# Unit order, selection rounds and gate sums moved between the input projection and the mixers of a two-layer hybrid decoder

## The chip, the core and the metric

The kernel runs on one NeuronCore of a Trainium2 chip. Its engines are TensorE (PE in the profile, with its weight loads shown apart as PEld), VectorE (DVE), ScalarE (ACT) and GpSimd (POOL); SyncE (SP) issues most of the DMAs. The metric is the device time of one launch in microseconds (us). Each engine executes its instructions in one fixed order.

## The reference, cut to what matters

Two layers. In each, one input projection makes the columns of four parallel groups of heads, the groups are mixed over the tokens, one output projection and a gated MLP follow. There are 1024 prompt tokens and 8 sequences of 4 sample tokens with 2048 cached tokens each.

```python
h = rmsnorm(x, norm1_g) * (1 + sc1) + sh1
p = split_cols(h @ w_in)                  # lru, diff, dsa, idx, gla columns
# A: RG-LRU recurrence over p["lru_x"], gated by p["lru_gate"]
# B: differential attention, q and k rotated (rope)
# C: sparse attention: index scores, exact 256 largest keys per query, q and k rotated
idx, valid = dsa_select(iq, iw, ik, q_pos, k_pos, 256)
o_c = dsa_attend(q_c, k_c[idx], v_c[idx], valid)
# D: gated linear attention; b is the running sum of log alpha in a chunk
b = cumsum(log_a / 16);  att = sum_k q k exp(b_t - b_s);  o = att @ v + (q exp(b)) @ S
x = x + g1 * (concat(o_a, o_b, o_c, o_d) @ w_out)
x = x + g2 * mlp(...)
```

The samples run B and C over their paged caches, and C needs its own selection of 256 keys per sample query.

## The kernel before

All activations of the projection are float32 split in two parts, so that 24 matmuls make one output tile. The projection runs unit by unit, 256 columns of `w_in` each. A `nat_unit` (queries, keys and values that later steps want by token) runs 9 token tiles through `dense_n` (L471); its queries and keys are rotated by `rope`: two VectorE instructions (L499 and L503) and two on GpSimd (L501, L502). A `t_unit` (features on partitions) runs 6 pieces of 384 or 288 columns through `dense_c` (L451). The units before were, in order: misc, idx_q, lru_x, lru_gate, dsa_q, dsa_k, dsa_v, diff_q, diff_k, diff_v, gla_v, gla_q with gla_k, gla_g.

Between the tiles `background()` lets side streams take steps: `idx_prompt` (index scores of the prompt), then `topk_prompt`, which finds the exact 256th largest score of each query by bisection with counts over all keys (L799 on VectorE, the upper 16 bits into `tkb`, the lower 16 into `tku`) and ends with the mask `mk` (L872); also `sample_index`, `rg_lru` and `sample_select`, the samples' own bisection, here called sel, whose round on VectorE holds the pair L967 and L969 (`srep`). `mk` of the last block, 128x1024, is the end of `topk_prompt`.

After the projection come the mixers. `gla()` (linear attention) goes first, in two halves of the prompt: `decays(half)` loads the 16 gate columns `ga`, multiplies by `wa2` (L1727), forms the log (ACT, L1730 to L1733, DVE L1734, L1736) and the running sum `gb` (scan, L1743); `operands(half)` loads q, k and v and makes the terms `gl`; `chunks(half)` does the attention in chunks of 128 tokens: PE L1700, and DVE L1711 into `gatt`. With it runs `samples()`, half a step for each of gla's steps, and sel, a step for every second. Each of the 16 sequences of the samples (8 for diff, 8 for dsa) has a group of keys (`samp_keys`: PE transposes L1334, scores L1340, mask L1343) and of values (`samp_values`, L1363; `samp_merge`). Then `prompt()` runs the prompt's attention with 0.8 sample steps for each of its own, and what is left of the samples runs alone; the last `out_t` (L1263) ends the prompt's part. The output projection (L451) follows and needs all the mixes.

The order of the instructions on an engine is not that of the code: a scheduler places each when its inputs are expected, and the streams decide what is available. Two further constants matter:

```python
SELH = 1    # projection: one step of sel per tile
SELM = 2    # gla: one step of sel per two of gla's
KA = 0.5    # sample steps per step of gla
while kind == "dsa" and advance(sel): yield     # samples(): the rest of sel
```

Of the kernel before, what the change touches and what calls it, by code (L numbers as in the profile page):

```python
# [22 lines left out]
D = 1024  # L23
# [21 lines left out]
SELH = 1  # L45
# [26 lines left out]
def _const_tables():  # L72
    """Tables and 0/1 masks that depend on shapes alone, one float32 array of 128 rows."""
# [67 lines left out]
def trunk(ctx, tc, io, out, dbg=None, depth=DEPTH, stop=99):  # L141
# [31 lines left out]
    def advance(gens, n=1):  # L173
        """n steps of the first streams of the list that are not done; False when none is left."""
# [9 lines left out]
    def pipeline(gens, depth):  # L184
        """the streams one after another, up to depth of them at once, a step of each per step, oldest first."""
# [20 lines left out]
    def evac(dst, src, ratio=(1, 1)):  # L206
        """PSUM to SBUF on ScalarE or VectorE in turns."""
# [91 lines left out]
            # half the convolution: silu(2 z) = z (1 + tanh(z))  # L299
# [17 lines left out]
    def ada(adap, l, u0, u1, nb=2, ne=1, nk=8):  # L317
        """units of 512 columns of the modulation, in pieces of nk * 128 rows and 1024 / nk columns."""
# [27 lines left out]
    def add_square(x, k, c, acc, tmp):  # L346
        """acc += x^2 for the features of tile k, chunk c of the tokens."""
# [13 lines left out]
    def rstd_chunk(get, acc, c):  # L361
# [3 lines left out]
        # 1 / sqrt(v), v = sum / D + eps: ScalarE's value, then a Newton step  # L365
# [9 lines left out]
    def split(hi, lo, y, bias, k):  # L375
        """hi + lo = y + bias, lo on VectorE or GpSimd in turns."""
# [8 lines left out]
    def norm_chunk(get, x, acc, c, A, mod, base, hi, lo):  # L385
        """hi + lo = modulated norm of x, chunk c of the tokens."""
# [16 lines left out]
    def part(wp, c, z):  # L403
        """tile for part z of [features, tokens], chunk c of the tokens."""
# [7 lines left out]
    def raw_piece(rp, aps, width, i, n, nr):  # L412
        """rows of piece i of n of a [1024, width] block of weights; aps: list of (column, AP)."""
# [12 lines left out]
    def unit(wp, rp, aps, width, n=2, first=None):  # L426
        """hi and lo of a block of weights, [128, 8, width]."""
# [10 lines left out]
    def split2(parts_, c, g, raw):  # L438
        """the parts of two tiles of features, chunk c of the tokens."""
# [4 lines left out]
    def dense_c(w, j, h, c, order=range(8)):  # L444
        """out^T[m, t] = sum_k w[k, m] h[k, t] for 128 columns m and chunk c of the tokens."""
# [16 lines left out]
    def dense_n(w, i, h):  # L462
        """out[t, m] = sum_k h[k, t] w[k, m] for token tile i, 256 columns."""
# [12 lines left out]
    def add_residual(x, m, c, p, gate, mod):  # L476
        """x += gate * p for 128 features m and token chunk c."""
# [11 lines left out]
    def rope(dst, src, i, n, d, tmp, rope_t):  # L489
        """dst[n, heads * d] = rotary of src (SBUF, natural rows of token tile i)."""  # L490
# [15 lines left out]
    # the scores' scales go into the queries, with their signs turned (minima for maxima)  # L506
# [60 lines left out]
    # the prompt's query blocks 2.. of the index: ScalarE counts by signs (2 * count - n) in those of ACT_BLK  # L567
# [11 lines left out]
    # rows of the caches: 4 tokens each; token (g*128+p)*4+j of sequence b lies in row idx[p, g, b]  # L579
# [33 lines left out]
    for l in range(depth):  # L613
# [8 lines left out]
        stt["gla_a"] = dr.tile([16, T], F32, name=f"stt_a{l}")  # L622
        mixg = [dr.tile([2, 128, T], F32, name=f"mix{l}_{k}") for k in range(4)]
# [9 lines left out]
        # ================= input projection =================  # L633
# [5 lines left out]
        def background():  # L639
# [5 lines left out]
            if count[0] % SELH == 0:  # L645
                advance(sel)
# [56 lines left out]
        def dup(dst, src, nh, d, key):  # L703
            """[n, nh, d] in two float32r parts, laid out (hi, hi, lo, lo) for queries, (hi, lo, hi, lo) for keys."""
# [7 lines left out]
        def stack_t(dst, srcs, idr=None):  # L712
            """dst[:, i*128:] = transpose of srcs[i], four to a PSUM bank."""
# [57 lines left out]
        def topk_prompt(tk):  # L771
            """Bisection over the bits of the float, the upper 16 first on the truncated values (order and
            comparisons with such thresholds are kept by truncation), then the lower 16 of those that share
            the upper ones. mk becomes 0 where chosen, -NEG elsewhere; ties in the order of the keys."""
# [32 lines left out]
            # thresholds of at least 0 end in zeros: the bfloat16 moved up by less than its spacing never equals  # L807
            # one, nor do those below 0, which end in ones. No bias of ScalarE's is subnormal.
# [390 lines left out]
        while advance(late) or advance(side):  # L1199
            pass  # L1200
# [1042 lines left out]
```

## Time and profile before

| | |
|---|---|
| median of 3 runs (lowest, highest) | 3935.86 us (3932.43, 3936.16) |
| the profiled execution | span 3915.6 us, 66494 instructions |
| PE / PEld busy | 3549.8 / 3202.2 us |
| DVE / ACT / POOL busy | 2461.3 / 1510.5 / 1387.5 us |
| layer 0, input projection from the top-k's first count | 275 to 562 us |
| layer 0, gla / prompt's mixers / samples alone | 562 to 743 / to 1058 / to 1077 us |
| layer 1, projection from the first count, gla | 2213 to 2500, to 2664 us |

Only the span has times of single instructions; the median lies 20.3 us above it. Busy shares are means over stages that have different limits, so the rows further below are taken by stage.

### The profile page before, as it was taken

Reading aid. Unit: us, or ns where it says so; the run is one execution under the profiler, and the core shown is the slowest. Engines: PE = TensorE matmul, PEld = TensorE weight load, DVE = VectorE, ACT = ScalarE, POOL = GpSimd, SP = SyncE. Lnnn points to the kernel's source line nnn. Section 1 sums busy time; section 2 is a strip of 40 time slices with the busy share of each in tenths; the row PEclk is TensorE's granted clock in tenths of the full one; section 3 lists DMA queues with packets and bytes.
Section 4 is the critical chain, followed back from the end, with each engine's and each line's share of the span. In section 5 each row is a group of like instructions: output and inputs, shape, how many; then the busy total and the mean of one; then the engine's idle time right before and its main releaser. Section 6 shows DMA issues by size and latency. Waiting matters only on the chain.

```text
span 3915.6 us, 66494 instructions
## 1 busy us (share of the span) xinstructions
PE 3549.8 (91%) x26004; PEld 3202.2 (82%) x26004; DVE 2461.3 (63%) x5614; ACT 1510.5 (39%) x3058; POOL 1387.5 (35%) x1241
## 2 busy tenths in 40 slices
PE   5998867899898999999979988688997899999998
PEld 3887765577788999999979877556786899999997
DVE  6379989676445454445553999996753545555555
ACT  4345644376533211211243556535763322112122
POOL 2344226534233222222323642564333222323231
PEclk7999988999999999999989999899998999999999
DMA  6542334546431333321113222546546011111111
GB/s 223 158 129 87 112 116 144 181 131 187 165 103 44 98 103 94 96 76 44 55 65 89 87 87 79 155 150 195 150 155 207 28 44 44 49 39 54 44 44 56
DMA packets 351155, 407.77 MB, mean 104 GB/s; under 512 B 93455, under 2 KB 294909, under 8 KB 350682
## 3 DMA queue, kind: packets, MB, share of 16 engines
q1 hardware_dynamic: 311930, 265.09, 22.5%
q0 software_dynamic: 38912, 138.43, 11.1%
q8 instruction: 205, 3.36, 0.4%
q14 instruction: 108, 0.88, 0.1%
HBM read 354.32 MB, written 58.04 MB: 105 GB/s over the span
## 4 chain that ended last, share of the span: by engine, by line
PE 66%; DVE 19%; DMA 4%; ACT 4%; issue 4%; POOL 1%; SPq 1%; another core or an unknown queue 0%; DVEq 0%; ACTq 0%; POOLq 0%
PE d L451 32%; PE m L2082 13%; PE m L1601 3%; PE d L471 2%; DVE tkb L799 2%; PE d L1334 2%; DVE tku L799 2%; PE e L1340 2%; PE e L1363 2%; PE m L1596 1%; PE d L330 1%; PE g L1700 1%; PE m L719 1%; DVE nat L499 1%; DMA xn<-in_x_prompt_dram 1%
## 5 line engine op out<-in xcount | busy, mean ns | idle before, releaser
L451 PE MATMUL d<-h,wh 128*128 128x384 f32 (+1 forms) x5856 | 1413.2, 327 | 69.2 <-ACT wh L434 26.2
L451 PEld LDWEIGHTS d<-h,wh 128*128 128x128 f32 x5856 | 1038.8, 192 | 86.2 <-ACT wh L434 31.5
L451 PE MATMUL d<-h,wl 128*128 128x384 f32 (+1 forms) x2928 | 947.4, 327 | 3.6 <-POOL wl L435 3.6
L451 PEld LDWEIGHTS d<-h,wl 128*128 128x128 f32 x2928 | 559.5, 191 | 7.8 <-POOL wl L435 6.7
L435 POOL TENSOR_TENSOR wl<-wr,wh 128x1024 fp32r<-128x1024 f32 (+1 forms) x172 | 376.7, 2208 | 357.5 <-ACT wh L434 345.5
L471 PE MATMUL d<-wh,h 128*128 128x256 f32 (+1 forms) x2304 | 462.5, 297 | 34.0 <-ACT nat L664 18.1
L480 DVE SCALAR_TENSOR_TENSOR xT<-m,mod,xT 128x384 f32<-128x384 f32 (+1 forms) x480 | 273.1, 572 | 228.8 <-PE m L2082 228.3
L471 PEld LDWEIGHTS d<-wh,h 128*128 128x128 f32 (+1 forms) x2304 | 372.0, 192 | 54.6 <-ACT nat L664 22.7
L2082 PE MATMUL m<-mh,wdh 128*128 128x384 f32 (+1 forms) x1056 | 349.2, 331 | 0.4 <-DVE xT L480 0.4
L2163 POOL TENSOR_TENSOR ml<-z,mh 128x384 fp32r<-128x384 f32 x132 | 133.5, 1031 | 605.7 <-ACT mh L2162 605.7
L2082 PE MATMUL m<-ml,wdh 128*128 128x384 f32 (+1 forms) x1056 | 343.3, 325 | 0.0
L2082 PE MATMUL m<-mh,wdl 128*128 128x384 f32 (+1 forms) x1056 | 342.1, 325 | 0.0
L471 PE MATMUL d<-wl,h 128*128 128x256 f32 (+1 forms) x1152 | 339.8, 295 | 0.0
L434 ACT CAST wh<-wr 128x1024 fp32r<-128x1024 f32 (+1 forms) x172 | 157.9, 955 | 238.7 <-PE d L451 174.5
L2134 DVE COPY fs<-G 128x2 f32<-128x2 f32 x44 | 50.9, 1158 | 285.2 <-ACT G L2130 285.2
L471 PEld LDWEIGHTS d<-wl,h 128*128 128x128 f32 (+1 forms) x1152 | 221.7, 192 | 8.0 <-issue 5.7
L2130 ACT COPY G<-d 128x384 f32<-128x384 f32 x132 | 57.1, 443 | 418.1 <-PE d L451 387.5
L2082 PEld LDWEIGHTS m<-mh,wdh 128*128 128x128 f32 x1056 | 199.6, 189 | 9.3 <-issue 7.0
L2082 PEld LDWEIGHTS m<-ml,wdh 128*128 128x128 f32 x1056 | 199.2, 189 | 1.5 <-issue 1.2
L2082 PEld LDWEIGHTS m<-mh,wdl 128*128 128x128 f32 x1056 | 199.3, 189 | 0.0
L2072 POOL TENSOR_TENSOR wdl<-wr,wdh 128x1024 fp32r<-128x1024 f32 x44 | 105.0, 2418 | 263.8 <-ACT wdh L2071 263.8
L1334 PE MATMUL d<-c_ident,kv 128*128 128x128 f32 x1024 | 171.8, 291 | 10.6 <-ACT s_wT L210 4.0
(532 smaller groups left out, 6740.4 us busy)
## 6 DMA issues: line engine op xcount, KB each, us to landing
adaw<-in_w_ada_dram SPq DMA_DIRECT2D x96, 512.0 KB
wr<-in_w_in_dram SPq DMA_DIRECT2D x48, 512.0 KB
wr<-in_ffn_w_gate_dram SPq DMA_DIRECT2D x44, 512.0 KB
wr<-in_ffn_w_up_dram SPq DMA_DIRECT2D x44, 512.0 KB
wr<-in_ffn_w_down_dram SPq DMA_DIRECT2D x44, 512.0 KB
xd<-xT SPq DMA_DIRECT2D x16, 528.0 KB
wr<-in_w_out_dram SPq DMA_DIRECT2D x32, 256.0 KB
mix<-mx SPq DMA_DIRECT2D x24, 256.0 KB
```

Of the source, the lines that this page charges most:

```text
L434: act.copy(hi[:, ks, :width], raw[:, :, :width])
L435: pool.tensor_tensor(lo[:, ks, :width], raw[:, :, :width], hi[:, ks, :width].bitcast(F32), op=sub)
L451: pe.matmul(pd, lhsT=w[a][:, k, j * 128:j * 128 + 128], rhs=h[b][c][:, k, :], start=(q == 0), stop=(q == 23))
L471: pe.matmul(pd[:n, :256], lhsT=h[b][c][:, k, t0:t0 + n], rhs=w[a][:, k, :], start=(q == 0), stop=(q == 23))
L480: dve.scalar_tensor_tensor(x[:, m, t0:t0 + n], p[:, :n], mod[:, gate + m, 0:1], x[:, m, t0:t0 + n], op0=mult, op1=add)
L799: dve.tensor_scalar(scratch[:, :n], src[:, s], thr[:, j:j + 1], None, op0=OP.is_ge, op1=add, accum_out=cnt[:, j:j + 1])
L1334: pe.transpose(pm[:, z_ * 128:z_ * 128 + 128], kg[:, j, f * 128:f * 128 + 128], ident)
L1340: pe.matmul(pd[32 * j:32 * j + 32, c], lhsT=Q[:, f, b_].rearrange("p c t -> p (c t)"), rhs=kt[:, j, f, :], start=(f == 0), stop=(f == 1))
L1601: pe.matmul(po[:, 64 * z:64 * z + 64], lhsT=wT[:, x * 128:x * 128 + 128], rhs=vn[:, kb, :], start=(kb == 0), stop=(kb == i))
L2072: pool.tensor_tensor(lo[:, z_, :], raw, hi[:, z_, :].bitcast(F32), op=sub)
L2082: pe.matmul(pd, lhsT=a, rhs=b, start=(n == 0), stop=(n == len(ops) - 1))
L2163: pool.tensor_tensor(ml[:, cs], z[:, cs], mh[:, cs].bitcast(F32), op=sub)
```

## The change

Four edits. (1) `SELH` goes, and with it the step of sel in `background()`. (2) The units after lru_gate now run as gla_q with gla_k, gla_g, gla_v, diff_q, diff_k, diff_v, dsa_q, dsa_k, dsa_v. (3) `decays` leaves `gla()` and becomes `gla_decays()`, a side stream of the projection, which writes `b` to memory (`stt_b`), from where `operands` loads it; the division by 16 goes from VectorE to ScalarE. (4) gla's first step, which issues its loads, runs ahead of the constants of the other mixers. Comments are dropped as well.

```diff
-SELH = 1
@@ background
             count[0] += 1
-            if count[0] % SELH == 0:
-                advance(sel)
@@ new side stream of the projection
+        def gla_decays():
...
+                for half in range(2):
...
+                    sp.dma_start(aT[:, :W], stt["gla_a"][:, g0])
...
+                        pe.matmul(pd[:, :W // 2], lhsT=wa2, rhs=aT[:, cs], start=True, stop=True)
+                        act.activation(la[:, cs], pd[:, :W // 2], AF.Identity, bias=V["gba"][:, 0:1])
+                    yield
+                    act.activation(ex[:, :W], la[:, :W], AF.Abs)
+                    act.activation(ex[:, :W], ex[:, :W], AF.Exp, scale=-1.0)
+                    act.activation(ex[:, :W], ex[:, :W], AF.Ln, bias=1.0)
+                    yield
+                    dve.scalar_tensor_tensor(la[:, :W], la[:, :W], 0.0, ex[:, :W], op0=OP.min, op1=sub)
+                    act.activation(la[:, :W], la[:, :W], AF.Copy, scale=1.0 / 16.0)
...
+                    dve.tensor_tensor_scan(ex[:, :W], rm[:, :W], la[:, :W], 0.0, op0=mult, op1=add)
+                    sp.dma_start(stt["gla_b"][:, g0], ex[:, :W])
@@ units
-        side += [sample_index(), rg_lru()]
-        for name in ("dsa_q", "dsa_k", "dsa_v", "diff_q", "diff_k", "diff_v", "gla_v"):
-            nat_unit(name)
+        side += [sample_index(), gla_decays(), rg_lru()]
         t_unit([("gla_q0", 128), ("gla_k0", 128)], [(0, col("gla_q"))], 256)
         t_unit([("gla_g0", 128), ("gla_g1", 128)], [(0, col("gla_g"))], 256)
+        for name in ("gla_v", "diff_q", "diff_k", "diff_v", "dsa_q", "dsa_k", "dsa_v"):
+            nat_unit(name)
@@ operands
-                bT = G[half]["b"]
+                bT = gl.tile([128, HW], F32, name="gb")
+                sp.dma_start(bT[:, :W], stt["gla_b"][:, g0])
@@ gla
-            yield from decays(0)
             yield from operands(0)
-            yield from both(chunks(0), decays(1), gates(0))
+            yield from both(chunks(0), gates(0))
@@ mixers
         ggen, sgen, pgen = [gla()], [samples()], [prompt()]
+        advance(ggen)
...
+        hm = {k: const("hm" + k, where=sm).rearrange("p (f c) -> p f c", f=2) for k in ("diff", "dsa")}
...
```

The constants of lambda and of the samples, which stood ahead of gla, now stand where the last lines show `hm`.

What this does to the engines' order is seen at three places. On VectorE in layer 0, late in the bisection of the lower 16 bits (`tku` counts), before:

```order
L799 TENSOR_SCALAR tku,cnt<-mk,tcd 128x640
L799 TENSOR_SCALAR tku,cnt<-mk,tcd 128x768
L1124 SCALAR_TENSOR_TENSOR la_5242<-la_5242,lth_5008 128x1056
L1137 MEMSET lav 128x8
L799 TENSOR_SCALAR tku,cnt<-mk,tcd 128x1024
L967 STREAM_TRANSPOSE srep<-scnt 128x32
L1125 MEMSET la_5242 128x1
L969 ISA srep,spc<-srep,c_agrp 128x32
```

The same three counts there after the change (line numbers are two lower):

```order
L498 TENSOR_TENSOR nat<-rraw,c_rope 128x256
L797 TENSOR_SCALAR tku,cnt<-mk,tcd 128x640
L797 TENSOR_SCALAR tku,cnt<-mk,tcd 128x768
L965 STREAM_TRANSPOSE srep<-scnt 128x32
L502 TENSOR_TENSOR nat<-nat,rtm 128x256
L797 TENSOR_SCALAR tku,cnt<-mk,tcd 128x1024
L967 ISA srep,spc<-srep,c_agrp 128x32
L967 ISA spc 128x1
L502 TENSOR_TENSOR nat<-nat,rtm 128x256
```

The rotations of dsa_q and dsa_k now stand among the last counts, where none stood. Counted over both orders, the rotation's instructions between the first count and the last `mk` go from 46 to 72 in layer 0 and from 38 to 72 in layer 1; the rounds of sel in the same stretch stay (21 and 23 before, 23 and 22 after).

On VectorE around the last `mk` of layer 0, before (`lp` belongs to lambda):

```order
L872 TENSOR_SCALAR mk<-tkb 128x1024
L1029 TENSOR_TENSOR sth<-sth,sdf 128x1
L1236 TENSOR_REDUCE ls<-lp 128x2
L1025 TENSOR_SCALAR snc<-sth 128x1
L1238 TENSOR_TENSOR nlam<-ls 128x1
```

and after, where `gl`, `gke` and `geb` are operands of gla's first half:

```order
L1739 COPY geb<-gqe 128x4
L1751 TENSOR_TENSOR gke<-gke,gk 128x512
L1768 TENSOR_TENSOR gl_6067<-gl_6067,gk 128x4x64
L1769 TENSOR_TENSOR gl_6067<-gl_6067,gq 128x4x64
L870 TENSOR_SCALAR mk<-tkb 128x1024
L1768 TENSOR_TENSOR gl_6113<-gl_6113,gk 128x8x32
L1769 TENSOR_TENSOR gl_6113<-gl_6113,gq 128x8x32
```

gla's operands have moved up to the end of the top-k. On TensorE at the end of layer 0's mixers, before, from the last `out_t` to the output projection:

```order
L1263 MATMUL m<-c_ident,oa_dsa 128x128
L1340 MATMUL e<-KT,s_Q 32x128 x8
L1343 LDWEIGHTS c_emat
L1343 MATMUL e<-selb,c_emat 128x128
L1363 MATMUL e<-kv,s_wT 32x256 x16
L1354 MATMUL d<-c_ident,s_S 128x128 x4
L1372 MATMUL d<-s_nz,c_ident 32x8 x4
L1363 MATMUL e<-kv,s_wT 32x256 x16
```

and after, of which the first and the last rows of the part that is new are given:

```order
L1275 MATMUL m<-c_ident,oa_dsa 128x128
L1342 MATMUL e<-KT,s_Q 32x128 x8
L1345 LDWEIGHTS c_emat
L1345 MATMUL e<-selb,c_emat 128x128
L1365 MATMUL e<-kv,s_wT 32x256 x16
L1356 MATMUL d<-c_ident,s_S 128x128 x4
L1336 MATMUL d<-c_ident,kv 128x128 x8
...
L1345 MATMUL e<-selb,c_emat 128x128
L1365 MATMUL e<-kv,s_wT 32x256 x16
L1356 MATMUL d<-c_ident,s_S 128x128 x4
L1374 MATMUL d<-s_nz,c_ident 32x8 x4
```

One whole sequence's keys (72 matmuls in four groups, each closed by `c_emat`) and one more group of values stand behind the prompt's last output; layer 1 has the same. On TensorE, from the first to the last matmul of the prompt's index scores, layer 0 has 288 matmuls of `dense_c` and 264 of `dense_n` before and 552 of `dense_c` after; layer 1 has 219 and 364 before, 507 and 67 after.

## Rows read from the trace of the kernel before

**Rows 1.** The page, part 1: busy time of each engine.
```profile
PE 3549.8 (91%) x26004; PEld 3202.2 (82%) x26004; DVE 2461.3 (63%) x5614; ACT 1510.5 (39%) x3058; POOL 1387.5 (35%) x1241
```
**Rows 2.** Busy time by stretch; columns start:end, length, engines, PE's granted clock, DMA.
```profile
275.00:562.00 287.00, 242.85 (x1631) 218.30 (x1630) 275.48 (x771) 150.50 (x309) 108.45 (x108) 0.94 0.27 85
562.00:620.00 58.00, 29.02 (x185) 21.33 (x186) 44.27 (x148) 31.55 (x62) 28.91 (x41) 0.68 0.65 191
620.00:735.00 115.00, 101.62 (x835) 69.48 (x833) 100.08 (x281) 36.36 (x79) 72.97 (x98) 0.91 0.47 144
735.00:1040.00 305.00, 287.12 (x2847) 222.83 (x2840) 188.98 (x481) 201.14 (x469) 117.89 (x101) 0.98 0.53 162
1058.00:1078.00 20.00, 10.20 (x127) 5.15 (x126) 10.97 (x20) 10.49 (x19) 7.94 (x5) 0.82 0.80 275
2213.00:2500.00 287.00, 232.88 (x1534) 208.47 (x1532) 276.95 (x790) 156.14 (x317) 108.24 (x104) 0.92 0.30 92
2500.00:2540.00 40.00, 22.04 (x197) 15.07 (x197) 35.70 (x110) 22.64 (x44) 30.41 (x37) 0.77 0.70 213
2540.00:2665.00 125.00, 106.28 (x886) 72.73 (x886) 107.96 (x310) 41.77 (x91) 76.85 (x102) 0.90 0.49 150
```
**Rows 3.** TensorE alone, within the index scores of layer 0: L451, then L471.
```profile
205.84:209.99 4.15, 4.15 (x24) 4.09 (x24) 1.00 0.50 140
240.63:243.66 3.03, 3.03 (x24) 2.91 (x24) 1.00 0.68 201
```
**Rows 4.** VectorE's groups by line, 290 to 575 us: busy, mean ns, idle before.
```profile
L799 DVE TENSOR_SCALAR_CACHE_REDUCE tku<-mk,tcd 128x384 uint16<-128x384 uint16 (+1 forms) x64 | 60.0, 938 | 0.3
L499 DVE TENSOR_TENSOR nat<-rraw,c_rope 128x256 f32<-128x256 f32 (+1 forms) x22 | 16.0, 727 | 0.5 <-issue 0.5
L503 DVE TENSOR_TENSOR nat<-nat,rtm 128x256 f32<-128x256 f32 (+1 forms) x24 | 10.6, 441 | 0.0
L969 DVE CUSTOM_DVE_ANT_0 srep<-srep,c_agrp 128x32 f32<-128x32 f32 x24 | 7.8, 329 | 0.1
```
**Rows 5.** The same view, 2200 to 2500 us.
```profile
L499 DVE TENSOR_TENSOR nat<-rraw,c_rope 128x256 f32<-128x256 f32 (+1 forms) x25 | 13.1, 525 | 0.1
L503 DVE TENSOR_TENSOR nat<-nat,rtm 128x256 f32<-128x256 f32 (+1 forms) x25 | 10.9, 438 | 0.2
```
**Rows 6.** VectorE's groups by line, 620 to 735 us.
```profile
L212 DVE COPY KT<-d 128x512 f32<-128x512 f32 x15 | 10.2, 682 | 0.2 <-PE d L1334 0.2
L1389 DVE TENSOR_TENSOR s_e<-s_e,s_M 32x20 f32<-32x20 f32 x1 | 0.5, 540 | 0.0
```
**Rows 7.** One line's durations, min/median/max: the division by 16.
```profile
L1736 DVE TENSOR_SCALAR gla<-gla x4: 383/429/450, 580.3 to 2535.9; 128x512 f32<-128x512 f32 x2, 128x544 f32<-128x544 f32 x2
```
**Rows 8.** The chain that ended last, 540 to 640 us: start, length, what.
```profile
561.14 0.59 issue
567.64 3.89 DMA ga<-stt_a
589.47 3.08 DVE gl L1789 x4
612.91 0.62 DVE gatt L1711
```
**Rows 9.** TensorE's groups by line, whole span.
```profile
L1334 PE MATMUL d<-c_ident,kv 128*128 128x128 f32 x1024 | 171.8, 291 | 10.6 <-ACT s_wT L210 4.0 <-issue 1.7 <-DVE s_wT L212 1.7
L1340 PE MATMUL e<-KT,s_Q 128*32 128x128 f32 x2048 | 133.8, 289 | 26.4 <-DVE KT L212 18.0 <-ACT KT L210 7.2 <-DVE snc L1025 1.1
```
**Rows 10.** TensorE's timeline around the last `out_t` of layer 0.
```profile
1054.52 0.23 PE L1343 MATMUL e<-selb,c_emat 128*128 128x128 bf16 x1
...
1057.79 0.23 PE L1343 MATMUL e<-selb,c_emat 128*128 128x128 bf16 x1
...
1059.86 0.23 PE L1343 MATMUL e<-selb,c_emat 128*128 128x128 bf16 x1
...
1077.37 1.62 PE L451 MATMUL d<-h,wh 128*128 128x384 f32 x4 [1.00 <-DVE s_oT L1416]
```

More of the change, by code (lines that the diff above doesn't have):

```diff
@@ L622, in trunk @@
         stt["gla_a"] = dr.tile([16, T], F32, name=f"stt_a{l}")
+        stt["gla_b"] = dr.tile([128, T], F32, name=f"stt_b{l}")
         mixg = [dr.tile([2, 128, T], F32, name=f"mix{l}_{k}") for k in range(4)]
@@ L1265, in out_t @@
                 yield mx, f
-        spool = tc.tile_pool(reuse_waits="tile", name="sp", bufs=2, side="right")
-        sm = spool.__enter__()
-        hm = {k: const("hm" + k, where=sm).rearrange("p (f c) -> p f c", f=2) for k in ("diff", "dsa")}
-        emat = const("emat", BF, sm, side="right").rearrange("p (b c) -> p b c", b=8)
-        newmask = const("newmask", where=sm, parts=32)
-        sel4 = const("sel4", where=sm)
-        sapool = tc.tile_pool(reuse_waits="tile", name="sa", bufs=1, side="right")
-        sa = sapool.__enter__()
-        oTs = {}
         def samp_prep(kind):
@@ L1664, in gla, with constants @@
                     gl.tile([128, w], F32, tag=tag, name=tag, bufs=n)
-            lmask = const("lmask", where=gl).bitcast(U32)
-            lms = [lmask[:, 64 * i:64 * i + 64] for i in range(8)]
-            qsel = const("qsel", where=gl).rearrange("p (b c) -> p b c", b=8)
-            ghead = const("ghead", where=gl)
-            wa2 = gl.tile([16, 128], F32, name="wa2")
-            sp.dma_start(wa2, io["gla_wa2"][l])
+            lms, gc = [], {}
+            def constants():
+                gc["ghead"] = const("ghead", where=gl)
+                lmask = const("lmask", where=gl).bitcast(U32)
+                lms.extend(lmask[:, 64 * i:64 * i + 64] for i in range(8))
+                gc["qsel"] = const("qsel", where=gl).rearrange("p (b c) -> p b c", b=8)
             og = gl.tile([128, 8, 256], F32, name="oa_gla")
@@ L1694, in intra @@
                                            rc[:, None].to_broadcast([128, 4, nb, mm_]),
-                                           ghead[:, :, None, None].to_broadcast([128, 4, nb, mm_]), op=mult)
+                                           gc["ghead"][:, :, None, None].to_broadcast([128, 4, nb, mm_]), op=mult)
                         bds.append(bd)
@@ L1758, in operands @@
                     sp.dma_start(vn[:32, 4, :], st["gla_v"][TP:, :])
+                if not half:
+                    constants()
                 act.activation(qT[:, :W], qT[:, :W], AF.Copy, scale=32.0 ** -0.5)
@@ L1850, in recur_samples @@
                 qb = gl.tile([128, 8, 32], F32, name="gqb")
-                dve.tensor_tensor(qb, qe[:, None, 512:].to_broadcast([128, 8, 32]), qsel, op=mult)
+                dve.tensor_tensor(qb, qe[:, None, 512:].to_broadcast([128, 8, 32]), gc["qsel"], op=mult)
                 yield
@@ L1950, in trunk @@
         ggen, sgen, pgen = [gla()], [samples()], [prompt()]
+        advance(ggen)
+        nlam = vecp.tile([128, 1], F32, name="nlam")
+        with tc.tile_pool(reuse_waits="tile", name="lm", bufs=1) as lm:
+            lq = lm.tile([128, 4, 32], F32, name="lq")
+            for i, key in enumerate(("diff_lq1", "diff_lk1", "diff_lq2", "diff_lk2")):
+                a = io[key][l]
+                sp.dma_start(lq[:, i, :], bass.AP(tensor=a.tensor, offset=a.offset, ap=[[0, 128], [1, 32]]))
+            lp = lm.tile([128, 2, 32], F32, name="lp")
+            dve.tensor_tensor(lp, lq[:, 0::2, :], lq[:, 1::2, :], op=mult)
+            ls = lm.tile([128, 2], F32, name="ls")
+            dve.tensor_reduce(ls, lp, axis=AX.X, op=add)
+            act.activation(ls, ls, AF.Exp)
+            dve.tensor_tensor(nlam, ls[:, 1:2], ls[:, 0:1], op=sub)
+            dve.tensor_scalar(nlam, nlam, -lam_init, None, op0=add)
+        cvec = vecp.tile([128, 1], F32, name="cvec")
+        dve.tensor_tensor(cvec, m1c, nlam, op=mult)
+        dve.tensor_tensor(cvec, cvec, m0c, op=add)
+        gsub = vecp.tile([128, 1], F32, name="gsub")
+        dve.tensor_scalar(gsub, V["diff_subln_g"], 1.0 - lam_init, None, op0=mult)
+        spool = tc.tile_pool(reuse_waits="tile", name="sp", bufs=2, side="right")
+        sm = spool.__enter__()
+        hm = {k: const("hm" + k, where=sm).rearrange("p (f c) -> p f c", f=2) for k in ("diff", "dsa")}
+        emat = const("emat", BF, sm, side="right").rearrange("p (b c) -> p b c", b=8)
+        newmask = const("newmask", where=sm, parts=32)
+        sel4 = const("sel4", where=sm)
+        sapool = tc.tile_pool(reuse_waits="tile", name="sa", bufs=1, side="right")
+        sa = sapool.__enter__()
         n = 0
```

65 lines of the change are left out of this document (18 added, 47 removed).

## Prediction

> **What bounds the kernel now.** By the whole span TensorE is the bound: it is busy 91% of it, VectorE 63% [rows 1]. That is a mean over stages, so I read busy time by stretch next [rows 2]. From the first count of the top-k to the end of the projection, VectorE is busy 275.5 of 287 us in layer 0 and 277.0 of 287 in layer 1, TensorE 242.9 and 232.9: here VectorE sets the end. At the start of the mixers both engines have holes: of 58 us VectorE is idle 13.7 and TensorE 29.0 (layer 0), of 40 us 4.3 and 18.0 (layer 1). In the rest of gla VectorE leads no more than by its 100.1 of 115 us (108.0 of 125 in layer 1), level with TensorE. In the prompt's mixers TensorE is the bound, 287 of 305 us. After the last `out_t` the samples run alone for 19 us with TensorE half idle. So a microsecond of VectorE's work is worth a microsecond between the first count and the end of gla, and a microsecond of TensorE's before the first count and in the prompt's mixers.
>
> What VectorE does in its saturated stretch is seen by line [rows 4]: counts of 938 ns, then the rotation's two instructions, 727 and 441 ns. The chain of work shows what the hole of layer 0 is made of [rows 8]: the last `mk` is done at about 561, then the gate columns are loaded (567.6 to 571.5), the log and the running sum follow, the terms `gl` begin at 589.5, and the first masked copy into `gatt` comes at 612.9.
>
> **The change, part by part.** I follow each layer to three ends: first count, end of gla, start of the output projection.
>
> First count. It waits for the index scores, which come tile by tile between the projection's matmuls, with TensorE full. The tiles among them change from `nat_unit` to `t_unit`. Twenty-four matmuls took 4.15 us with 384 columns and 3.03 us with 256 [rows 3]; a third of a `t_unit`'s pieces has 288, so a mean matmul is 4.15 / 24 x 352 / 384 = 0.158 us against 0.126. Layer 0 swaps 264 matmuls: 264 x 0.032 = +8.5 us. Layer 1 gets 288 of the long ones for 297 of the short: 45.6 - 37.5 = +8.1. Bounds: nothing, if VectorE's earlier work could fill the time, and +10; VectorE has nothing to fill it with, since its rotations are what went away from there.
>
> VectorE from there to the end of gla. By the order, 26 of the rotation's instructions come into the stretch in layer 0 (13 pairs) and 34 in layer 1 (17 pairs). A pair is 0.727 + 0.441 = 1.17 us [rows 4] and 0.525 + 0.438 = 0.96 us [rows 5]: +15.2 and +16.4. Before the change these ran where VectorE had room. The decays only move within this stretch: their log and scans cost VectorE the same ahead of the last `mk` as behind it. Only the division by 16 leaves, twice 0.43 us [rows 7]; ScalarE has the room, 150 of 287 us [rows 2]. The four writes and four loads of `stt_b` go through SP, where they stand among others; gla's first load is due long before VectorE is free. Since gla takes some ten steps fewer, five sample steps drop out of it: by the order two or three copies of `KT` (0.68 us each) and a dozen small merge instructions (0.54 us at the dearest) [rows 6] go behind the end of gla. Together -6, bounds -2 and -9. Sum: 8.5 + 15.2 - 6 = +17.7 in layer 0, 8.1 + 16.4 - 6 = +18.5 in layer 1.
>
> Sel costs nothing in this sum, because it doesn't move. The code takes its step out of `background()`, but between the first count and the last `mk` the order has 23 and 22 of its rounds where 21 and 23 stood. A round's longest piece is 0.33 us [rows 4], so one or two more or less is within a microsecond or two.
>
> Against this stands the hole. With the decays done and the loads ahead of the constants, `gl` and `gke` stand in the order next to the last `mk`, so the load, the log and the scan (561 to 612) no longer stand between. VectorE's idle time of 13.7 and 4.3 us [rows 2] I give back whole. In the rest of gla VectorE is idle 14.9 and 17.0 us, mostly for one TensorE answer after another; the second half's decays were part of that mix, so I give back a third, 5.0 and 5.7. The bounds are nothing and all of it. End of gla: 17.7 - 18.7 = -1.0 in layer 0; 18.5 - 10.0 = +8.5 in layer 1.
>
> The end of the mixers. The samples lose five steps in gla, and about fourteen more because the rest of sel now uses up steps of the samples' stream; so one whole sequence comes after the prompt's last output. A group of keys took 2.07 us there alone and 3.27 between the prompt's matmuls (from mask to mask: 1054.52, 1057.79, 1059.86) [rows 10]; four groups are 8.3 to 13.1 us, and the DMA engines are already 80% busy there [rows 2], so I take 12. In exchange the sequence's matmuls leave the stretches ahead: for the keys 171.8 / 32 + 133.8 / 32 = 9.6 us [rows 9], with 32 sequences in both layers. About half left gla, where TensorE had room; the other half, 5 us, shortens the prompt's mixers. Net +7 a layer, bounds -1.3 (8.3 - 9.6) and +20 (a second tail as long as the first, nothing saved). What is late next is the output projection, which stood at 1077.4 [rows 10] behind the last merge.
>
> Sum: -1.0 + 8.5 + 2 x 7 = +21.5 us. The profiled span of 3915.6 would become 3937; the median lies 20.3 above the span, so 3957.
>
> The rest of both layers (output projection, MLP) is untouched. Here a rule can be weighed. The row: TensorE's granted clock was 0.68 of full in the 58 us behind layer 0's projection and 0.77 in the 40 us of layer 1, where TensorE stood half idle [rows 2]; between its two levels, 1.2 and 2.4 GHz, that is a mix. The Trainium skill (TensorE: Matmul & The Clock Gate, section Why this matters for your kernels) advises against holes between bursts of matmuls, since the clock drops after one. By that rule closing the hole would also give TensorE its clock back, while the longer tail, at 0.82 now, would lose some. The row agrees that holes and a low clock go together; what the clock is worth is a rival below, because in these 58 us VectorE's chain, and not TensorE, is what the next step waits for.
>
> **The rivals.**
>
> The hole pays for everything (faster). Place: the start of gla and gla itself. If all of VectorE's idle time there goes, 13.7 + 14.9 and 4.3 + 17.0 us, and the tail nets -1.3 a layer, the sum is 17.7 - 28.6 + 18.5 - 21.3 - 2.6 = -16 us: 3920. For it: the first masked copy waits 52 us after the last `mk` now [rows 8], TensorE is idle 29 us there. Against it: in those 52 us VectorE is mostly at work that still has to be done, and the first half's chunks alternate between engines as before. It decides once a layer gets back more than its 18 us of added work plus the tail's 7.
>
> It cancels (the same). TensorE's matmuls in the hole, 29.0 and 22.0 us at 0.68 and 0.77, would be 9.3 and 5.1 us shorter at full clock. If TensorE's share of the chain there is that large, the sum is 21.5 - 14.4 = +7: 3943. For it the low clock, against it that VectorE waits there for ScalarE and loads as well.
>
> Nothing comes back (slower still). If the loads of `b`, q and k, which SP issues behind the writes of dsa_v and six loads of heads, land late, the hole stays, in another place: 17.7 + 18.5 + 14 = +50: 3986. For it, these loads do stand behind the unit that now ends last; against it, the order has `gl` ahead of the last `mk`.
>
> That the change doesn't do what it says holds for sel, as above. Did its rounds really leave VectorE's saturated stretch, some 22 rounds a layer would go, 7 us each for the one piece of 0.33 alone, and they would come back in gla at 87% busy; I give this no chance of its own, as the order is fixed.
>
> **How the numbers follow.** The measurement tells about 0.2%, 7.9 us, from no change. The forecast has 0.42, with an own range of 3946 to 3972, the hole that stays 0.08, so slower 0.50. Cancelling has 0.20. The faster rival and what lies between it and cancelling have 0.30: the added work is counted out of a fixed order, but how much idle time returns is a guess, and it is the largest term. The range reaches from the faster rival to the hole that stays, less a little at either end: 3920 to 3984.
>
> **What would show it.** In the profile after: the first count some 8 us later in each layer; the rotations at the same price among `tku` counts, and VectorE again above 95% up to the last `mk`, which comes 30 to 45 us later than 561 and 2500, since the decays and first operands now stand ahead of it too; the first masked copy within 20 us of it, against 52; gla ending near 742 and near 2672; between last `out_t` and output projection about 31 us instead of 19. Wrong would be a first count that is not later, rotations that fit into TensorE's waits, a gla stretch with VectorE above 95%, or a tail of 20 us.

## The result, and the profile after

The changed kernel takes 3982.56 us (3979.7 to 3988.24, 4 runs) against 3934.14 for the kernel before on the same chip: ratio 1.0128, 95% interval 1.0113 to 1.0142, 48 us slower. Forecast were 3957, 21 us slower. The direction and the range held; the loss is more than twice the forecast.

The page after, part 1, answers to [rows 1]:

```profile
PE 3552.5 (89%) x26004; PEld 3198.9 (80%) x26004; DVE 2434.8 (61%) x5610; ACT 1512.6 (38%) x3062; POOL 1380.9 (35%) x1241
```

The engines do the same work; the time is idle time. Busy time by stretch (start:end, length, PE, PEld, DVE, ACT, POOL, PE's granted clock, DMA), with the stretches cut at the changed kernel's own events (first count, last mask, gla, after the last `out_t`, and layer 1's first count to last mask), answers to [rows 2]:

```profile
281.00:589.00 308.00, 233.00 (x1655) 208.92 (x1654) 297.49 (x830) 169.71 (x340) 130.84 (x144) 0.90 0.30 91
589.00:620.00 31.00, 23.10 (x106) 16.51 (x106) 26.29 (x100) 6.79 (x19) 21.76 (x28) 0.67 0.44 139
620.00:735.00 115.00, 92.44 (x757) 63.30 (x756) 95.32 (x275) 38.86 (x84) 66.22 (x89) 0.90 0.45 138
1063.00:1107.00 44.00, 25.20 (x263) 14.40 (x263) 15.24 (x29) 15.84 (x29) 20.87 (x16) 0.76 0.63 227
2248.00:2560.00 312.00, 223.46 (x1566) 197.80 (x1564) 302.98 (x843) 166.12 (x336) 129.38 (x147) 0.87 0.29 87
```

VectorE is busy 97% of the stretch up to the last mask (96% before), and the stretch has grown from 292 to 308 us in layer 0 and from 287 to 312 us in layer 1. (The last mask of layer 0 before is done at 567.1; the 562 of the table of stages is five us short.) The rotations there, by line from 295 to 575 us, answer to [rows 4]:

```profile
L498 DVE TENSOR_TENSOR nat<-rraw,c_rope 128x256 f32<-128x256 f32 (+1 forms) x36 | 23.1, 641 | 0.0
L502 DVE TENSOR_TENSOR nat<-nat,rtm 128x256 f32<-128x256 f32 (+1 forms) x36 | 17.9, 498 | 0.0
```

A pair costs 0.641 + 0.498 = 1.14 us, against 1.17 in the forecast. The hole behind the last mask is gone on VectorE: 26 of 31 us are busy. For TensorE it has moved ahead of the mask. In the 29 us up to the last mask of layer 0, before and after (same columns):

```profile
538.00:567.00 29.00, 13.92 (x74) 13.13 (x73) 27.97 (x64) 5.30 (x14) 7.75 (x8) 0.80 0.31 94
560.00:589.00 29.00, 0.88 (x2) 0.29 (x2) 28.94 (x43) 9.64 (x18) 23.29 (x18) 0.50 0.63 167
```

The projection is over by then and the samples have not begun, so TensorE has 0.9 us of work where it had 13.9; in layer 1 it has none where it had 12.8.

What is new as well is the stretch 1063 to 1107: 44 us between the prompt's last output and the output projection, where there were 19 us. Its timeline on TensorE (start, length, line, operation, count, idle time ahead with its releaser):

```profile
1063.37 0.27 PE L1275 MATMUL m<-c_ident,oa_dsa 128*128 128x128 f32 x1
...
1064.82 0.23 PE L1345 MATMUL e<-selb,c_emat 128*128 128x128 bf16 x1
...
1071.90 0.82 PE L1336 MATMUL d<-c_ident,kv 128*128 128x128 f32 x4 [2.26 <-DVE s_wT L211]
...
1077.46 0.23 PE L1345 MATMUL e<-selb,c_emat 128*128 128x128 bf16 x1
1078.15 1.06 PE L1336 MATMUL d<-c_ident,kv 128*128 128x128 f32 x8 [0.46 <-issue]
1087.54 1.08 PE L1342 MATMUL e<-KT,s_Q 128*32 128x128 f32 x16 [8.33 <-ACT KT L209]
...
1093.69 0.29 PE L1345 MATMUL e<-selb,c_emat 128*128 128x128 bf16 x1
...
1104.97 0.44 PE L1413 MATMUL d<-c_ident,s_om 128*128 128x128 f32 x2 [0.49 <-ACT s_om L1409]
```

It is the whole sequence that the order showed, and it runs at less than half the pace I gave it: from mask to mask (L1345) its four groups of keys, with the values of the sequence before among them, take from 1064.8 to 1093.7, where I had 12 us. Why TensorE waits 8.33 us for one copy is on ScalarE's timeline:

```profile
1077.80 0.83 ACT L440 CAST h<-mixr 128x768 fp32r<-128x768 f32 x1 [1.32 <-issue]
1081.11 0.83 ACT L440 CAST h<-mixr 128x768 fp32r<-128x768 f32 x1 [2.47 <-DMA mixr<-mix]
1086.17 0.83 ACT L440 CAST h<-mixr 128x768 fp32r<-128x768 f32 x1 [4.23 <-DMA mixr<-mix]
1086.91 0.58 ACT L209 COPY KT<-d 128x512 f32<-128x512 f32 x1
```

The copy stands behind casts of the output projection, which wait for their loads.

Why a sequence is left over at all is seen at the other end, where the samples begin. The timeline of SP's queue at the start of layer 0's mixers:

```profile
587.37 0.34 SPq L1722 DMA_DIRECT2D gb<-stt_b  x1
591.45 0.27 SPq L1193 DMA_DIRECT2D out_dram<-lrw  x1
...
592.42 0.28 SPq L1196 DMA_DIRECT2D out_dram<-lrw  x1
595.37 1.78 SPq L1872 DMA_DIRECT2D ggg<-stt_gla_g  x2
597.20 0.42 SPq L219 DMA_DIRECT2D c_hmdiff<-in_const_dram  x1
...
599.55 0.43 SPq L875 DMA_DIRECT2D s_q<-st_diff_q  x1
```

The samples' constants (`c_hmdiff`) and queries (`s_q`) are issued behind `lrw`, the outputs of rg_lru. What the queue waited for between 577 and 597 us (who waited, for what: total us, times, longest):

```profile
SPq L1722 <- DVE gl L1764: 9.9, 1, 9.9
SPq L1193 <- ACT lrw L1192: 3.7, 1, 3.7
SPq L1872 <- DVE gl L1776: 2.9, 1, 2.9
SPq L1872 <- DVE gkn L211: 1.3, 1, 1.3
```

So `lrw` is not the only thing ahead of the constants: the longest wait is that of the load of `b` for gla's second half, which edit (3) brought in. Before, rg_lru's outputs had long left. The same two issues in the kernel before (first and last start in us, one per layer), and then after:

```profile
L1164 SPq DMA_DIRECT2D out_dram<-lrw x2: 277/298/318, 548.7 to 2482.1; - x2
L220 SPq DMA_DIRECT2D c_hmdiff<-in_const_dram x2: 453/658/864, 563.8 to 2498.9; - x2
```

```profile
L1196 SPq DMA_DIRECT2D out_dram<-lrw x2: 276/276/277, 592.4 to 2563.2; - x2
L219 SPq DMA_DIRECT2D c_hmdiff<-in_const_dram x2: 362/391/420, 597.2 to 2564.6; - x2
```

In layer 0 rg_lru ends 44 us later and the constants come 33 us later. The samples move about as much: in layer 0 their first matmul goes from 573.5 to 603.1, their last from 1076 to 1105.

### The profile page after: what moved, and what is told of

It is laid out like the page before. It is cut to its first block, busy times and chain, and to the rows that moved or that the text cites. A ratio compares the mean times of both kernels' runs of the same rounds, so it can differ in the third digit from the quotient of the medians.

```text
span 3977.9 us, 66528 instructions
## 1 busy us (share of the span) xinstructions
PE 3552.5 (89%) x26004; PEld 3198.9 (80%) x26004; DVE 2434.8 (61%) x5610; ACT 1512.6 (38%) x3062; POOL 1380.9 (35%) x1241
## 4 chain that ended last, share of the span: by engine, by line
PE 63%; DVE 13%; DMA 3%; issue 2%; ACT 2%; POOL 1%; SPq 0%; another core or an unknown queue 0%; ACTq 0%; DVEq 0%; POOLq 0%
PE d L450 31%; PE m L2086 13%; PE m L1603 3%; PE d L1336 3%; PE e L1342 2%; PE m L1598 2%; PE e L1365 2%; DVE tku L797 1%; DVE tkb L797 1%; PE m L717 1%; DMA wr<-in_w_out_dram 1%; PE s L1559 1%; PE d L470 1%; DVE gatt L1714 1%; DMA mixr<-mix 1%
## 5 line engine op out<-in xcount | busy, mean ns | idle before, releaser
L1336 PE MATMUL d<-c_ident,kv 128*128 128x128 f32 x1024 | 171.7, 292 | 12.8 <-DVE s_wT L211 5.6
```

The lines of the kernel that those rows point to most:

```text
L1336: pe.transpose(pm[:, z_ * 128:z_ * 128 + 128], kg[:, j, f * 128:f * 128 + 128], ident)
```

## The experiments

The kernel before took about 3934 us on some of the chips and 3895 to 3900 on others, so each time is compared with that of the kernel before in its own group, and stages of two kernels only where both ran on one chip or the difference is large.

**The edits apart.** First the changed kernel with the units in their old order, everything else kept:

```diff
+        for name in ("dsa_q", "dsa_k", "dsa_v", "diff_q", "diff_k", "diff_v", "gla_v"):
+            nat_unit(name)
         t_unit([("gla_q0", 128), ("gla_k0", 128)], [(0, col("gla_q"))], 256)
         t_unit([("gla_g0", 128), ("gla_g1", 128)], [(0, col("gla_g"))], 256)
-        for name in ("gla_v", "diff_q", "diff_k", "diff_v", "dsa_q", "dsa_k", "dsa_v"):
-            nat_unit(name)
```

> The changed kernel with the units in their old order; the other edits stay. Against 3934 before and 3983 changed. Theory U (the later end of the top-k, by rotations and index scores, pushes everything behind it): the last mask is done within 8 us of before in layer 0, and the time comes back to 3935 to 3950. Rival G (with the decays done early, gla takes the engines first, GpSimd issues its products before the samples' first gathers, and the samples, which begin late, end late): the masks come early again, but the gathers still stand behind gla's first chunk and a sequence stays behind the prompt's last output; 3955 to 3970.

Measured: 3970.19, ratio 1.0095 (1.0076 to 1.0113), 37 us above before. The last mask of layer 0 is done at 562.9, as early as before, and still the samples begin at 601.9 and end at 1092.6. Theory U falls for this kernel.

Then the changed kernel with the decays back in gla (`decays(0)` and `decays(1)` as before, no `gla_decays`):

```diff
-        side += [sample_index(), gla_decays(), rg_lru()]
+        side += [sample_index(), rg_lru()]
...
+            yield from decays(0)
             yield from operands(0)
```

> The changed kernel with the decays back in gla; the new unit order, the missing step of sel and the order of the loads stay. Theory U: 3970 to 3983, since the last mask stays 20 us late or more. Rival G: the first gathers go ahead of gla's products, the tail of layer 0 is the old one (under 22 us), and the time is 3945 to 3962.

Measured: 3954.9, ratio 1.0057 (1.0036 to 1.0077), 22 us above. More than half of the loss goes with this one edit. rg_lru's outputs leave at 551.1 again and the tail of layer 0 is the old one, 17 us; that of layer 1 is still 41, with the constants at 2544.0, near the last mask (2550.4).

The kernel before with only that edit:

```diff
-        side += [sample_index(), rg_lru()]
+        side += [sample_index(), gla_decays(), rg_lru()]
...
-            yield from decays(0)
             yield from operands(0)
-            yield from both(chunks(0), decays(1), gates(0))
+            yield from both(chunks(0), gates(0))
```

> The kernel before with only the decays moved into the projection. Theory U: the hole behind the last mask closes and nothing else changes: 3915 to 3934. Rival G: the samples begin some 30 us after gla instead of with it, one sequence stays behind the prompt's last output in each layer (tail 35 us or more instead of 19): 3945 to 3970.

Measured: 3964.08, ratio 1.0086 (1.0065 to 1.0107), 31 us above. gla ends earlier (727.2 in layer 0, against 743.0 before), the samples begin later (596.6 against 573.5), and the loss goes with the samples. And the kernel before with only the new order of units (the first diff turned round):

> The kernel before with only the new order of the units. Theory U: the last mask 18 to 25 us later in each layer, and most of the loss is here: 3965 to 3985. Rival G: the mask is as late, but the samples still start with gla; 3945 to 3965.

Measured: 3974.88, ratio 1.0109 (1.0089 to 1.0129), 42 us above. The edits don't add up: 31 and 42 alone, 48 with all four, 22 with the other three.

**What holds the samples up.** The first three of these times fell into the ranges of G, gla displacing the samples, or beside them; the fourth fell into that of U. But in every kernel with `gla_decays` ahead of rg_lru the samples' constants came right behind rg_lru's outputs. Theory M was formed from that, and tested by a swap of two names:

```diff
-        side += [sample_index(), gla_decays(), rg_lru()]
+        side += [sample_index(), rg_lru(), gla_decays()]
```

> The changed kernel with one swap: rg_lru stands ahead of gla_decays among the side streams of the projection. Theory M (the samples' constants and gathers wait, on SP and for memory, until rg_lru is done, and gla_decays has pushed that back by 40 us): rg_lru's outputs leave before 560 in layer 0, the constants are loaded by 580, the first gathers by 590, the tail is that of the kernel before, and the time is 3935 to 3960. Rival G (gla ready early takes the engines first whatever rg_lru does): the samples begin at 600 as now, 3970 to 3985.

Measured: 3905.03 against 3896.67, ratio 1.0023 (1.0014 to 1.0033), 8 us above before instead of 48. The two issues in this kernel:

```profile
L1196 SPq DMA_DIRECT2D out_dram<-lrw x2: 277/277/277, 553.0 to 2468.5; - x2
L219 SPq DMA_DIRECT2D c_hmdiff<-in_const_dram x2: 424/453/482, 578.2 to 2496.7; - x2
```

The first gathers came at 598.7, later than theory M said; the samples' first matmuls (581.9) wait for the constants and queries. The swap changes more than rg_lru's place: the last mask of layer 0 comes at 575.8, where the changed kernel has 589.0. A cleaner pair follows further below. The swap with the units in their old order:

> The same swap with the units in their old order. Theory M: samples and gla both start right behind the projection, 3905 to 3935. Rival G: 3955 to 3970, as without the swap. If only the unit order mattered: 3950 to 3970.

Measured: 3910.75, ratio 1.0039 (1.0025 to 1.0053), 14 us above. M's 3905 to 3935 was meant beside 3934, that is up to 29 us below before, and is missed. Once rg_lru is early, the old order of units is no better than the new one. Here the samples begin at 563.2 in layer 0, the earliest of all runs, and end only at 1068.1.

The strictest test keeps gla as it was and only puts the stream in front of rg_lru. The kernel before, with `gla_decays` as a side stream whose result nobody reads, gla making its own decays as ever:

```diff
-        side += [sample_index(), rg_lru()]
+        side += [sample_index(), gla_decays(), rg_lru()]
```

> The kernel before with gla_decays as a side stream ahead of rg_lru, its result unused; gla still makes its own decays, so nothing of gla comes earlier, and some 4 us of VectorE's work a layer are added. Theory M (rg_lru pushed back by the stream ahead of it holds up the samples' loads): rg_lru's outputs leave near 590 instead of 549, the samples' constants behind them, and the time is 20 to 45 us above before. Rival G (the early start of gla displaces the samples): within 10 us of before.

Measured: 3948.29 against 3897.93, ratio 1.0128 (1.0111 to 1.0145), 50 us above, a little more than M's 20 to 45. G can't explain this loss: nothing of gla is early here. The two issues:

```profile
L1198 SPq DMA_DIRECT2D out_dram<-lrw x2: 277/277/277, 584.3 to 2519.6; - x2
L220 SPq DMA_DIRECT2D c_hmdiff<-in_const_dram x2: 369/398/427, 585.0 to 2521.3; - x2
```

The constants follow rg_lru within 1 us in layer 0. gla is held up here too: its first masked copy comes at 619.6 (601.7 in the repeat of the kernel before, below), and layer 0 loses its time with no sequence left over, by everything being later. Two plain repeats on the chip of this run give the stages of the kernel before and of the changed one side by side.

> The changed kernel as it is, on the chip of this call, for its times beside the kernel before: some 45 to 50 us above it, with the samples' constants loaded 30 us late in both layers.

> The kernel before as it is, on the same chip, so that single stages can be compared within one chip: the samples begin 12 us behind the last tile of the projection, the tail is 17 us.

One time each, 3946.33 and 3888.47: 58 us apart, where the medians are 48 apart, so each stage below may be off by some us. In layer 0:

| us | before | changed | doubled decays | swap |
|---|---|---|---|---|
| rg_lru's last output issued | 544.9 | 594.1 | 584.3 | 553.0 |
| samples' constants issued | 559.1 | 598.9 | 585.0 | 578.2 |
| samples' first matmul | 568.9 | 605.4 | 590.4 | 581.9 |
| gla's last transpose | 739.0 | 738.9 | 758.2 | 741.5 |
| last `out_t` | 1045.7 | 1051.9 | 1067.3 | 1047.2 |
| samples' last matmul | 1063.8 | 1093.4 | 1086.4 | 1063.7 |

The swap is from another group of runs. From first to last matmul the samples take 495, 488, 496 and 482 us. Starts that were 36 and 22 us later came out as ends 30 and 23 us later; the 13 us of the swap did not come out at all.

**Is that a chain?** Two kernels leave out the last dsa sequence of the samples, the changed one and the one before:

```diff
+                    if kind == "dsa" and b_ == 7:
...
+                        obs.append(obs[-1])
+                        prev.append(samp_merge(kind, b_ // 4, E, nN, nz, obs, vs, oT))
+                        prev.append(samp_out(kind, oT))
+                        continue
```

> The changed kernel without the keys and values of the last dsa sequence of the samples (the results of the one before stand in for it). Theory C (the samples are a chain of 16 sequences of some 31 us each, from their first load to the output projection, and this chain ends the mixers): 45 to 65 us less in both layers together, 3920 to 3940. Rival T (only the part behind the prompt's last output counts): about as much here, 30 to 45 less, since there is a whole sequence in that tail.

> The kernel before without the same sequence. Theory C: 45 to 65 us less, as in the changed kernel: 3870 to 3890. Rival T: the sequence lies within the prompt's mixers, where it costs its share of TensorE, 10 to 14 us a layer, and of the tail little: 3905 to 3920.

Measured: the changed kernel 3908.29, ratio 1.0028 (1.0015 to 1.0041), 12 us above before instead of 48; the kernel before 3891.68, ratio 0.9987 (0.9976 to 0.9998), 5 us. Theory C falls for the time of the whole: in the kernel before, the samples do end 18 us earlier, with the last `out_t`, but the output projection then waits for its weights. Rival T's 14 to 29 us less are missed too. The projection's first matmul in layer 0:

```profile
1056.79 1.65 PE L451 MATMUL d<-h,wh 128*128 128x384 f32 x4 [11.12 <-ACT wh L434]
```

So in these two kernels the sequence costs (48 - 12) / 2 = 18 us a layer where it stands behind the prompt, and next to nothing within it.

The tail's dearness was tried by itself, with the last sequence's `KT` copies on VectorE alone:

```diff
-                    evac(kt[:, 2 * jj:2 * jj + 2].rearrange("p j f c -> p (j f c)"), pm)
+                    evac(kt[:, 2 * jj:2 * jj + 2].rearrange("p j f c -> p (j f c)"), pm,
+                         (0, 1) if kind == "dsa" and b_ == 7 else (1, 1))
```

> The changed kernel with the KT copies of the last dsa sequence on VectorE alone, so that none stands on ScalarE behind the output projection's casts of the mix, which wait for their loads. If that queue makes the tail dear (8.3 us of TensorE's wait in layer 0, 6.9 in layer 1), the time falls by 10 to 16 us against the changed kernel. Rival: the gathers set the pace of the tail, within 4 us of the changed kernel.

Measured: 3942.26, ratio 1.0112 (1.0095 to 1.0128), beside 3946.33 of the one run of the changed kernel on that chip. That is 4 us, not clear of the noise. The trace shows why: the wait only moved. In the same groups of layer 0 TensorE now waits for the copies on VectorE:

```profile
1071.82 1.66 PE L1343 MATMUL e<-KT,s_Q 128*32 128x128 f32 x16 [3.54 <-DVE KT L211]
...
1081.55 1.66 PE L1343 MATMUL e<-KT,s_Q 128*32 128x128 f32 x16 [6.14 <-DVE KT L211]
```

The copies stand there behind VectorE's part of the output projection's preparation (L441), and the tail of layer 0 is 45 us, beside 42 in the changed kernel on that chip.

**What stays after the swap.** The kernel before without the step of sel:

```diff
-            if count[0] % SELH == 0:
-                advance(sel)
```

> The kernel before with only the step of sel taken out of the projection's background. The prediction says that sel doesn't move, so nothing: within 8 us of before. Rival S (sel's steps, taken out of the samples' stream instead, put one sequence behind the prompt's last output in layer 0, as the order shows): 10 to 25 us above before.

Measured: 3908.07 against 3899.45, ratio 1.0027 (1.0017 to 1.0037), 9 us, between the two expectations. Sel's rounds stay where they were, but a sequence goes behind the prompt's last output in layer 0: last `out_t` at 1041.6, the samples' last matmul at 1075.2. The early decays alone, behind rg_lru:

> The kernel before with only the decays moved, as the third experiment, but with gla_decays behind rg_lru. Theory M: the 31 us of that experiment go, within 10 us of before or faster, since then nothing holds the samples up. Rival G (gla ready early displaces the samples): 15 to 35 us above before.

Measured: 3905.93, ratio 1.0022 (1.0012 to 1.0033), 6 us above instead of 31 with the same edit ahead of rg_lru (third experiment). This is the cleanest pair: in layer 0 the last mask (560.9 and 561.3), gla's first masked copy (591.8 and 592.1) and gla's end agree within 1 us, and rg_lru's outputs (545.5 and 590.8) and the constants behind them (559.0 and 591.1) differ. The tail of layer 0 is 37 and 38 us, so a sequence behind the prompt's last output is not by itself a loss: here the prompt ends earlier (1031.8) and the samples 18 us earlier than there (1069.1 and 1087.2). Two ways to begin the samples earlier, rg_lru ahead of sample_index too, and raised priorities for the samples' loads:

> The changed kernel with rg_lru ahead of sample_index and gla_decays. Theory M: rg_lru's outputs leave earlier still; as the fifth experiment or a few us better, -10 to +10 against before. If instead sample_index, now later, holds up sel and with it the dsa sequences: 15 to 30 above before.

> The fifth experiment with the samples' first constants, loads and gathers raised in the scheduler's priority, to begin the samples as early as memory allows. If their beginning still sets the end: 5 to 15 us below the fifth experiment, so at or under the time before. Rival: the output projection's weights, which a shorter samples' part has to wait for, set the end; as the fifth experiment, +5 to +12.

Measured: 3929.64, ratio 1.0085 (1.0068 to 1.0102), and 3921.2, ratio 1.0053 (1.0035 to 1.0071), 30 and 22 us above. In the first, rg_lru is done at 421.7 and the samples' constants still come only at 570.4:

```profile
L1196 SPq DMA_DIRECT2D out_dram<-lrw x2: 276/276/276, 421.7 to 2355.3; - x2
L219 SPq DMA_DIRECT2D c_hmdiff<-in_const_dram x2: 431/440/449, 570.4 to 2497.6; - x2
```

So an early rg_lru is needed and not enough: the constants then come with the end of the top-k (last mask at 569.4). Over all runs they come within 5 us behind rg_lru's last output where that is late, and within 11 us of the last mask, on either side, where it is early. The time of this kernel is the one that its expectation named second, sample_index holding up sel, and sel is late indeed. Its first and last round in layer 0, in the fifth experiment and here:

```profile
L965 DVE STREAM_TRANSPOSE srep<-scnt x47: 155/206/214, 412.2 to 695.9; 128x32 f32<-128x32 f32 x47
L965 DVE STREAM_TRANSPOSE srep<-scnt x47: 188/211/230, 547.3 to 786.5; 128x32 f32<-128x32 f32 x47
```

What of the 30 us is due to that was not separated. The second kernel, with the raised priorities, missed both of its expectations, and no run explains its 22 us. Neither start came earlier than that of the kernel before. Last, the swap with the step of sel put back:

```diff
+            if count[0] % SELH == 0:
+                advance(sel)
...
-        side += [sample_index(), gla_decays(), rg_lru()]
+        side += [sample_index(), rg_lru(), gla_decays()]
```

> The fifth experiment with the step of sel back in the projection's background, that is the change without its first edit and with rg_lru ahead of gla_decays. If the costs add up (8 us for the missing step of sel alone, 8 us for the fifth experiment), this one is within 4 us of the kernel before. Rival: the step of sel makes no difference here, since the fifth experiment has no sequence behind the prompt's last output; +4 to +12, from the later first count.

Measured: 3917.96 against 3895.53, ratio 1.0051 (1.0036 to 1.0066), 22 us above: neither expectation, and the costs of single edits don't add. No version that does the whole work was below the kernel before.

## Why the prediction was wrong in its size

Up to the end of gla the sum was right within 2 us a layer, by the stages of the two plain repeats, although two of its readings of the kernel before were off and the hole moved instead of closing.

- **First count.** Forecast +8.5 us in layer 0; it went from 271.5 to 282.2, +10.7, just above the upper bound of 10.
- **Last mask.** Forecast 30 to 45 us later; it went from 562.3 to 590.7, +28.4, and in layer 1 by 20 beyond the 36 by which the first count there is late. The rotations cost what [rows 4] said. I had put the last mask of the kernel before at 561, from a chain that leaves its short pieces out [rows 8]; its last instruction of that line starts at 566.6.
- **The hole.** First masked copy 8 us after the last mask (597.3 after 589.0), forecast within 20. The 52 us that the prediction set against it came from the chain [rows 8] as well: by its first instruction the copy came 39 us after the last mask (605.9 after 567.1). VectorE's idle time came back.
- **End of gla.** Forecast -1.0 and +8.5. Measured 739.0 to 738.9 in layer 0; in layer 1 2643.7 to 2681.2, +37.5, of which the layer entered some 30 late: +7.7.
- **The rule on the clock.** The granted clock was 0.67 in the 31 us behind the top-k and 0.76 in the 44 us of the tail, against 0.68 and 0.82 before: TensorE got no clock back there, and the tail lost some. Its hole was not closed but stood ahead of the last mask, with the clock at 0.50, the lower of the two levels, over those 29 us. That agrees with what the prediction took from the Trainium skill (TensorE: Matmul & The Clock Gate, section Why this matters for your kernels): the clock drops after a hole between bursts of matmuls.

The term that failed is the last one, "Net +7 a layer". From the end of gla to the end of the samples the changed kernel took 29.7 us more in layer 0 and 21.6 in layer 1, 51 instead of 14; within these two runs, 58 us apart, this is the whole of the error. Two sizes in it were wrong. The sequence in the tail was priced at 12 us, from groups of keys that the output projection's preparation did not hold up [rows 10]; with one whole sequence the tail grew from 18 us to 42 in layer 0 and to 34 in layer 1, and one wait for a copy alone was 8.33 us. The 5 us that I took off the prompt's mixers are not there: 28 of the 32 key transposes that went behind the last `out_t` in layer 0 had stood in gla, and the prompt's mixers got 6 us longer instead.

And the cause was misread. I had the sequence left over because gla has fewer steps and sel uses up steps of the samples' stream. That part is real, but small: 9 us with sel's step alone. The larger cause is a step of the prediction that says where the decays go and not what stands behind them: "The decays only move within this stretch: their log and scans cost VectorE the same ahead of the last `mk` as behind it." That their cost stays was no mistake; what they delay had no price. They became a stream ahead of rg_lru, whose last scan on VectorE went from 525 to 559, and whose outputs stand on SP ahead of the samples' constants. That the place of that stream is enough for the loss is shown: with its work added and nothing else changed the loss is 50 us, and with the early decays behind rg_lru instead of ahead of it 25 of 31 us come back, with gla and the top-k as early in layer 0. With the two names swapped in the changed kernel 40 of the 48 come back, part of which may be the earlier end of the top-k there. That the constants wait for rg_lru by the scheduler's plan of memory, and not by the mere order of SP's queue, was argued and not tried; the new loads of `b`, which SP also waited for, are a third candidate in the changed kernel, but the third experiment and the doubled decays show the late constants without such a wait.

What stays open: the new order of units costs 42 us alone (rg_lru is not late there; the top-k ends later and the samples' constants with it, 576.5 against 563.8 in layer 0) and nothing measurable once rg_lru stands first. Edit (4) was not tried alone. Each kernel gets its own order on all five engines, and the runs here don't separate these.

## What to carry to other kernels

When work is moved into a stream that runs in turn with others, price the stream behind it: what it delays, and what waits for that. Find the part of a stage that is long and thin, here the samples, 16 sequences over 490 us beside full engines, and ask first when it begins; starts that were 22 and 36 us later came out at its end almost whole, while 13 us did not, and 16 us gained at the end of gla (third experiment) did not show either. And single edits of a scheduled kernel don't add up: the one that looked dear alone (42 us) was free in other company.

## What was not expected

The output projection waits for its own preparation as soon as the mixers end earlier: with a sequence less, its first matmul came 11.1 us after TensorE was free, for the cast of a weight, and of 18 us gained in layer 0 8 were left. In the tail the DMA engines were busy 0.63 of the time at 227 GB/s, where the kernel before had 0.80 and 275 [rows 2].
